# Two sets of level tiles for the block inverses, with rotary, key and value buffers shared or shortened

## The chip, the cores and the metric

The kernel runs on one core of one Trainium2 chip. The metric is the device time of one execution in microseconds; of several runs the median counts. The profile is of one execution of its own, whose time is given beside its span.

## The reference

One layer of a hybrid encoder in float32: 1024 tokens of width 1024. A first projection feeds two mixers, whose outputs are joined by an output projection; then come cross-attention to 256 memory tokens and a SwiGLU. The change lies in the first mixers.

```python
# (A) windowed attention: 8 query heads, 2 key/value heads of width 64, +-128 tokens
q, k = _rope(q, positions), _rope(k, positions)      # two rotated halves of 32
scores = einsum(q, k in the band) * 64 ** -0.5       # softmax with a sink logit per head
o = p / denom @ v
# (B) bidirectional gated DeltaNet: 4 heads of width 128, two directions
lower = where(strict, (k * beta) @ k.T * decay, 0)   # per chunk of tokens
sol = triangular_solve(lower + eye, [v * beta, k * beta * exp(g)])
scan over the chunks: v_new = u - w @ state; o = qg @ state + qk @ v_new
                      state = state * g_last + kg.T @ v_new
```

## The kernel before

Weights are split on the fly into a high and a low fp32r part, and every projection is three matmuls in place of one (`pg`, L261). The program is written as a list of stages, and a scheduler sets the order of the instructions on each engine from the dependences and its own cost model; the text of the program sets only the order in which stages are offered to it, as three strings. Every engine runs its list in order; loads and stores are nearly all issued by SyncE (SP).

In the first string the four DeltaNet heads are projected, convolved and prepared (`prep`), and `base_inverse` inverts the 32 x 32 diagonal blocks of each chunk's triangular matrix for a pair of heads g (heads 0 and 1, then 2 and 3). It does so on VectorE in 60 small steps, after a mask on GpSimd (POOL, L528), and stores the blocks to `d_inv` (L543). The second string is the stage of this change. Its letters are: L, the levels of a head; G, a gate projection; A, a rotary projection (A4 the keys, A0 to A3 the queries); V, the values; W, two attention windows. The third is the scan over the chunks (`psc`, L785), with the memory's keys and values and the remaining windows in between; it reads what the levels stored to `d_pz`.

`levels(h)` joins the 32 x 32 inverses of a head into 64 x 64 and then 128 x 128 ones. It fetches the diagonal blocks by twenty small loads (L551) into five tiles: `m5`, and D5, D6, Z0, Z1, which hold 128 x 128 blocks per chunk, zero outside the blocks. These four are allocated once, zeroed by GpSimd (L719), and used by all four heads in turn; so a head's fetches wait until the head before has stored its Z tiles to `d_pz` (L610). For each half of the chunks it also loads `Ul` (L572), transposes it (L576), masks it into L5 and L6, and does four rounds of small matmuls (L585 and L591), each evacuated before the next.

`attn_proj` multiplies a projection with the sine (`sn`) and cosine (`rop`), brings the sine product to the other half of each head by four copies on SP (`rot`, L734), adds, splits into `qhi` and `qlo`, and stores these to `d_q` or `d_k`. `value_proj` copies the values to `vT` (L746), transposes them (`ptv`, L749) and splits them into `vhl`. `window_keys(g)` loads a key group's `khi` and `klo` (L679); a window loads its queries `qs` (L625), and its matmuls are `psw`, `ptw` and `pow`.

Of the kernel before, what the change touches and what calls it, by code (L numbers as in the profile page):

```python
# [10 lines left out]
F32 = mybir.dt.float32  # L11
F32R = mybir.dt.float32r
# [7 lines left out]
P = 128  # L20
S = 1024
D = 1024
KT = D // P
NT = S // P
HALF = 512
# [7 lines left out]

ORDER_1 = "D0 P0 D1 P1 D2 B0 P2 D3 P3 B1".split()
ORDER_2 = "L0 L1 G0 G1 A4 V A0 A1 L2 L3 W W W A2 A3 G2 G3 W".split()
ORDER_3 = ("M " + "s01 W K " * 5 + "s01 K " * 3 + "s01 V V").split()
# [37 lines left out]
def tile_hybrid_block(  # L76
# [16 lines left out]
    def f32(ap):  # L93
        return ap.bitcast(F32)

    def bc(ap, axis, shape):
        return ap.unsqueeze(axis).to_broadcast(list(shape))

    def split(hi, lo, src, scale=None, eng=None):

        if scale is None:
            nc.scalar.copy(hi, src)  # L102
            (eng or nc.vector).tensor_tensor(lo, src, f32(hi), ALU.subtract)  # L103
        else:
            nc.scalar.activation(hi, src, AF.Identity, scale=scale)
            nc.vector.scalar_tensor_tensor(lo, src, scale, f32(hi), ALU.mult, ALU.subtract)

    def pool(name, bufs, **kw):
        return tc.tile_pool(name=name, bufs=bufs, reuse_waits="tile", **kw)
# [39 lines left out]
    trp = p1.enter_context(pool("trp", 2, side="right"))  # L149
# [48 lines left out]
    def small():  # L198
        return ps.tile([P, 512], F32, tag="ps", name="ps")
# [11 lines left out]
    for hf in range(2):  # L211
        hi = hx.tile([P, KT, HALF], F32R, name=f"hhi{hf}")
        lo = hx.tile([P, KT, HALF], F32R, name=f"hlo{hf}")
        for j in range(4):
            t = 4 * hf + j
# [48 lines left out]
    def proj(src_cols, eng=None):  # L264
        whi, wlo = load_w(src_cols, KT, P, eng)
        pp = [pg.tile([P, 512], F32, tag="pg", name="pg") for _ in range(2)]
        gemm_b(whi, wlo, hT, pp)
        return pp
# [140 lines left out]
    def together(gens):  # L409

        gens = list(gens)
        while gens:
            gens = [g for g in gens if next(g, g) is not g]
# [132 lines left out]
    def levels(h):  # L546

        g, hh = h // 2, h % 2

        def fetch(dst, q, i, d):  # L550
            nc.sync.dma_start(dst, d_inv[g][i][d, hh, :, q].rearrange("c r s -> r c s"))  # L551

        m5 = tl_.tile([P, NT, 32], F32, tag="m5", name="m5", bufs=1)
        D5a, D6a, *Za = wide_sets[0]
        for q in range(4):
            r = slice(32 * q, 32 * q + 32)
            fetch(m5[r], q, 1, 1 - q % 2)
            fetch(D5a[r, :, r], q, 0, q % 2)
            fetch(D6a[r, :, r], q, 0, q // 2)
            for d in range(2):  # L560
                fetch(Za[d][r, :, r], q, 1, d)

        def part(b):
            c4 = slice(4 * b, 4 * b + 4)

            def wide(name):
                return tl_.tile([P, 4, P], F32, tag=name, name=name, bufs=2)

            L5, L6 = wide("L5"), wide("L6")
            D5, D6, Z = D5a[:, c4], D6a[:, c4], [z[:, c4] for z in Za]  # L570
            Ul = wide("Ul")
            nc.sync.dma_start(Ul, d_u[g][hh, c4].rearrange("c p n -> p c n"))  # L572
            yield
            p_ = small().rearrange("p (c n) -> p c n", c=4)
            for j in range(4):
                nc.tensor.transpose(p_[:, j, :], Ul[:, j, :], ident)  # L576
            nc.vector.tensor_tensor(L5, p_, bc(cm["m5"], 1, (P, 4, P)), ALU.mult)
            nc.vector.tensor_tensor(L6, p_, bc(cm["m6"], 1, (P, 4, P)), ALU.mult)

            def pair(lt, mv, dd, w):  # L580

                yield
                p_ = small()[:, 0:4 * w].rearrange("p (c n) -> p c n", c=4)
                for c in range(4):
                    nc.tensor.matmul(p_[:, c, :], lt[:, c, :], mv[:, c, :], start=True, stop=True)  # L585
                bs = tl_.tile([P, 4, 64], F32, tag="bs", name="bs", bufs=2)[:, :, 0:w]
                nc.scalar.copy(bs, p_)
                yield
                p_ = small()[:, 0:4 * w].rearrange("p (c n) -> p c n", c=4)
                for c in range(4):  # L590
                    nc.tensor.matmul(p_[:, c, :], dd[:, c, :], bs[:, c, :], start=True, stop=True)  # L591
                return p_

            p_ = yield from pair(L5, m5[:, c4, :], D5, 32)
            z5 = tl_.tile([P, 4, 32], F32, tag="z5", name="z5", bufs=2)
            nc.scalar.mul(z5, p_, -1.0)
            nc.vector.transpose(D6[32:64, :, 0:32], z5[0:32])
            nc.vector.transpose(D6[64:96, :, 96:128], z5[96:128])
            nc.vector.tensor_copy(Z[1][32:64, :, 0:32], z5[32:64])
            nc.vector.tensor_copy(Z[0][64:96, :, 96:128], z5[64:96])  # L600
            mov6 = tl_.tile([P, 4, 64], F32, tag="mov6", name="mov6", bufs=2)
            nc.scalar.copy(mov6[0:64], Z[1][0:64, :, 0:64])
            nc.vector.tensor_copy(mov6[64:128], Z[0][64:128, :, 64:128])
            nc.scalar.copy(Z[0][0:32, :, 32:64], z5[0:32])
            nc.scalar.copy(Z[1][96:128, :, 64:96], z5[96:128])
            p_ = yield from pair(L6, mov6, D6, 64)
            nc.scalar.mul(Z[0][0:64, :, 64:128], p_[0:64], -1.0)
            nc.vector.tensor_scalar(Z[1][64:128, :, 0:64], p_[64:128], -1.0, None, ALU.mult)
            for d in range(2):
                nc.sync.dma_start(d_pz[g][d][c4, :, hh, 1].rearrange("c p n -> p c n"), Z[d])  # L610

        together([part(b) for b in range(2)])
# [60 lines left out]
    keys, vhl = {}, None  # L673

    def window_keys(g):
        keys[g] = tw.tile([P, S], F32R, tag="khi", name="khi"), tw.tile([P, S], F32R, tag="klo", name="klo", bufs=1)
        for kk, src in zip(keys[g], d_k):
            for r in range(2):
                nc.sync.dma_start(f32(kk[64 * r:64 * r + 64]), src[64 * g:64 * g + 64, :])  # L679
# [23 lines left out]
    def issue(order, table):  # L703
        for o in order:
            table[o[0]](*(int(c) for c in o[1:]))

    issue(ORDER_1, {"D": delta_proj, "P": lambda h: prep(h, *kqv[h]), "B": base_inverse})
    pp_.close()
# [3 lines left out]
    ps = pgs.enter_context(pool("psl", 2, space=PSUM))  # L712
    tw = p12.enter_context(pool("tw", 2))
    tw.tile([P, 384], F32, tag="sc", name="sc", bufs=8)
    vhl = tw.tile([P, NT + 1, 2, 2, 64], F32R, tag="vhl", name="vhl", bufs=1)[:, 0:NT]
    tl_ = p1.enter_context(pool("tl", 2))
    wide_sets = [[tl_.tile([P, NT, P], F32, tag=f"{n}{i}", name=n, bufs=1) for n in ("D5", "D6", "Z0", "Z1")] for i in range(1)]
    for t in wide_sets[0]:
        nc.gpsimd.memset(t, 0.0)  # L719

    def attn_proj(ct):
        pp = proj(w_in[:, ct * P:(ct + 1) * P])
        dst = [t[ct * P:(ct + 1) * P, :] if ct < 4 else t for t in (d_q if ct < 4 else d_k)]
        for hf in range(2):
            sl = slice(hf * HALF, (hf + 1) * HALF)
            rop = trp.tile([P, HALF], F32, tag="rop", name="rop")
            sn = trp.tile([P, HALF], F32, tag="rot", name="sn")
            rot = trp.tile([P, HALF], F32, tag="rot2", name="rot2")
            nc.vector.tensor_tensor(sn, pp[hf], sinT[:, sl], ALU.mult)
            nc.vector.tensor_tensor(rop, pp[hf], cosT[:, sl], ALU.mult)  # L730

            for q in range(4):
                o = 32 * (q ^ 1)
                nc.sync.dma_start(rot[32 * q:32 * q + 32], sn[o:o + 32])  # L734
            nc.vector.tensor_tensor(rop, rop, rot, ALU.add)
            hl = [trp.tile([P, HALF], F32R, tag=t, name=t) for t in ("qhi", "qlo")]
            split(*hl, rop)
            for t, o in zip(hl, dst):
                nc.sync.dma_start(o[:, sl], f32(t))
# [13 lines left out]
    def gate_proj(h):  # L753

        pp = proj(w_in[:, 2304 + h * P:2304 + (h + 1) * P])
        for hf in range(2):
            gt = trp.tile([P, HALF], F32, tag="rop", name="gt")
            nc.scalar.activation(gt, pp[hf], AF.Silu)
            nc.sync.dma_start(d_gate[h * P:(h + 1) * P, hf * HALF:(hf + 1) * HALF], gt)

    issue(ORDER_2, {"A": attn_proj, "V": value_proj, "G": gate_proj, "L": levels, "W": next_windows})
    dump("d_q", d_q); dump("d_k", d_k); dump("d_gate", d_gate)
    p1.close()
# [439 lines left out]
    for e in range(EARLY):  # L1203
        f = 2 * e
# [320 lines left out]
```

## Time and profile before

| | us |
|---|---|
| median of 3 runs | 1550.36 (1548.67 to 1551.51) |
| profiled execution, time | 1555.78 |
| profiled execution, span | 1554.1 |
| TensorE busy | 1497.3 |
| VectorE busy | 1055.9 |
| ScalarE busy | 719.6 |
| GpSimd busy | 308.3 |

The mean granted TensorE clock is 0.983. In the views quoted below, PE is TensorE and PEld its weight loads, DVE VectorE, ACT ScalarE, POOL GpSimd, SP SyncE; SPq is the queue of SyncE, that is, its DMA issues. A row of the chain gives start, length, engine, tile and line. A row of a line's instructions gives the shortest, median and longest duration in ns and the start of the first and the last. A tile is named in the profile without its number, and D5 and D6 both read D there.

### The profile page before, as it was taken

To read this page: it belongs to the slowest core of one execution; us is meant where nothing else is said; L and a number is where in the kernel's file an instruction comes from. 1 tells how busy PE (TensorE), PEld (TensorE's weight loads), DVE (VectorE), ACT (ScalarE), POOL (GpSimd) and SP (SyncE) were. 2 spreads that over 40 slices of the span, in tenths; PEclk is the share of its full clock that TensorE was granted. 3 is DMA by queue.
4 is the path that set the end of the run, shared out by engine and by line. 5 is a ranking of instruction groups with operands and counts; after the bars stand their busy time and mean duration, and the time that the engine had idled before them with its cause. 6 is when DMAs were issued, how large, how long until landed. Compare 5 with 4: busy or idle time off the path is not lost.

```text
span 1554.1 us, 20931 instructions
## 1 busy us (share of the span) xinstructions
PE 1497.3 (96%) x7451; PEld 1258.1 (81%) x7451; DVE 1055.9 (68%) x1750; ACT 719.6 (46%) x1380; POOL 308.3 (20%) x305
## 2 busy tenths in 40 slices
PE   6999999898899999999999999999999999999998
PEld 5888888787899877888888777888888888888786
DVE  6777898766898766443447367776867554687665
ACT  6666552246556755454335574332323332454532
POOL 2000110000003201163102221433533333000021
PEclk9999999997999999999999999999999999999999
DMA  6244456867987584354213264344434334863354
GB/s 211 69 136 128 125 157 160 217 179 245 319 278 247 164 283 165 119 190 148 82 55 123 85 200 141 111 135 129 134 122 132 102 102 141 288 193 102 108 175 165
DMA packets 267366, 247.16 MB, mean 159 GB/s; under 512 B 39016, under 2 KB 204797, under 8 KB 267261
## 3 DMA queue, kind: packets, MB, share of 16 engines
q1 hardware_dynamic: 267261, 245.82, 50.7%
q8 instruction: 59, 0.97, 0.3%
q14 instruction: 46, 0.38, 0.1%
HBM read 173.65 MB, written 69.50 MB: 156 GB/s over the span
## 4 chain that ended last, share of the span: by engine, by line
PE 80%; DVE 6%; DMA 6%; ACT 3%; issue 2%; SPq 2%; POOL 0%; DVEq 0%; POOLq 0%; ACTq 0%
PE pg L261 13%; PE pmg L1016 10%; PE pD L1196 8%; PE pE L1196 8%; PE pA L1196 6%; PE pcq L261 6%; PE pdX L1386 6%; PE pdA L1386 4%; PE pB L1196 4%; PE psc L785 2%; PE pdX L1479 2%; PE pdD L1386 2%; DMA wraw<-in_w_ckv_dram 2%; PE pcs L1102 1%; PE pco L1128 1%
## 5 line engine op out<-in xcount | busy, mean ns | idle before, releaser
L102 ACT CAST whi<-wraw 128x1024 fp32r<-128x1024 f32 x108 | 113.5, 1051 | 173.3 <-PE pg L261 36.0
L103 DVE TENSOR_TENSOR wlo<-wraw,whi 128x1024 fp32r<-128x1024 f32 x78 | 95.5, 1225 | 77.7 <-ACT whi L102 75.0
L261 PE MATMUL pg<-hhi,whi 128*128 128x512 f32 x352 | 140.8, 401 | 0.2 <-DVE rop L730 0.2
L261 PE MATMUL pg<-hhi,wlo 128*128 128x512 f32 x352 | 140.2, 399 | 0.0
L261 PE MATMUL pg<-hlo,whi 128*128 128x512 f32 x352 | 139.9, 398 | 0.0
L1016 PE MATMUL pmg<-whi,b 128*128 128x512 f32 x384 | 118.4, 394 | 0.4 <-ACT b L102 0.4
L1196 PE MATMUL pA<-s,whi 128*128 128x512 f32 x352 | 109.5, 392 | 1.4 <-ACT m L1213 1.4
L103 POOL TENSOR_TENSOR wlo<-wraw,whi 128x1024 fp32r<-128x1024 f32 x30 | 73.8, 2460 | 143.3 <-ACT whi L102 143.2
L1016 PEld LDWEIGHTS pmg<-whi,b 128*128 128x128 f32 x384 | 71.3, 188 | 15.2 <-ACT b L102 1.3
L261 PEld LDWEIGHTS pg<-hhi,whi 128*128 128x128 f32 x352 | 67.3, 192 | 14.0 <-DVE rop L730 0.7
L261 PEld LDWEIGHTS pg<-hlo,whi 128*128 128x128 f32 x352 | 67.2, 191 | 13.2
L261 PEld LDWEIGHTS pg<-hhi,wlo 128*128 128x128 f32 x352 | 67.2, 191 | 13.1
L1196 PEld LDWEIGHTS pA<-s,whi 128*128 128x128 f32 x352 | 65.3, 188 | 15.2 <-ACT m L1213 2.0
L1386 PE MATMUL pdX<-dhl,whi 128*128 128x512 f32 x264 | 76.1, 390 | 1.5 <-DVE zv L1441 0.8
L1016 PE MATMUL pmg<-wlo,b 128*128 128x512 f32 x192 | 71.5, 392 | 0.0
L1196 PE MATMUL pA<-s,wlo 128*128 128x512 f32 x176 | 68.7, 392 | 1.1 <-DVE wlo L103 1.1
L102 ACT CAST whi<-araw 128x1024 fp32r<-128x1024 f32 (+1 forms) x36 | 35.4, 984 | 69.9 <-PE pdX L1386 27.6
L1273 POOL TENSOR_TENSOR act<-act,up 128x512 f32<-128x512 f32 x33 | 50.1, 1519 | 89.1 <-DVE up L1272 53.1
L103 DVE TENSOR_TENSOR wlo<-araw,whi 128x1024 fp32r<-128x1024 f32 (+1 forms) x36 | 40.8, 1133 | 38.4 <-ACT whi L102 38.3
L286 DVE SCALAR_TENSOR_TENSOR acc<-cp,cols,acc 128x1024 f32<-128x1024 f32 x48 | 61.5, 1282 | 1.5 <-ACT acc L284 0.8
L1386 PEld LDWEIGHTS pdX<-dhl,whi 128*128 128x128 f32 x264 | 49.3, 188 | 12.8 <-issue 1.1
L1246 DVE TENSOR_TENSOR sr<-sr,wraw 128x512 f32<-128x512 f32 x22 | 37.8, 1716 | 29.8 <-POOL sr L1245 29.8
(409 smaller groups left out, 3976.7 us busy)
## 6 DMA issues: line engine op xcount, KB each, us to landing
wraw<-in_w_gate_up_dram SPq DMA_DIRECT2D x52, 512.0 KB, 4.0
kv<-d_kv SPq DMA_DIRECT2D x32, 512.0 KB, 6.6
wraw<-in_w_in_dram SPq DMA_DIRECT2D x22, 512.0 KB, 5.5
b<-in_w_down_dram SPq DMA_DIRECT2D x20, 512.0 KB, 6.8
araw<-d_as SPq DMA_DIRECT2D x20, 512.0 KB, 3.8
pz<-d_pz SPq DMA_DIRECT2D x32, 256.0 KB, 6.8
wraw<-in_w_ckv_dram SPq DMA_DIRECT2D x16, 512.0 KB, 6.4
wraw<-in_w_out_dram SPq DMA_DIRECT2D x16, 512.0 KB, 4.3
```

The source lines that it names most:

```text
L102: nc.scalar.copy(hi, src)
L103: (eng or nc.vector).tensor_tensor(lo, src, f32(hi), ALU.subtract)
L261: nc.tensor.matmul(p_, w[:, k, :], ah[a][:, k, :], start=(k == 0 and i == 0), stop=(k == nk - 1 and i == 2))
L286: nc.vector.scalar_tensor_tensor(acc, cp[:, t:t + S], taps[t], acc, ALU.mult, ALU.add)
L785: nc.tensor.matmul(out[:, d, h, :], lt[:, d, h, :], rt[:, d, h, :], start=True, stop=True)
L1016: nc.tensor.matmul(pp[t], act[a][:, k, tt], w_[:, kk, :], start=(k == 0 and i == 0), stop=(k == KT - 1 and i == 2))
L1102: nc.tensor.matmul(pp[:, t2_, :], q[a][:, ct, tt], kr_[b_][:, ct, :], start=(j == 0 and i == 0), stop=(j == 1 and i == 2))
L1196: nc.tensor.matmul(out_, w[a][:, k, :], xx[b_][:, k, :], start=(start and k == 0 and i == 0), stop=(k == HK - 1 and i == 2), skip_group_ch ...
L1246: nc.vector.tensor_tensor(s[1], s[0], a_[:, 0:HK], ALU.subtract)
L1273: nc.gpsimd.tensor_tensor(o_, o_, up, ALU.mult)
L1386: nc.tensor.matmul(banks[t], a[:, k - k0, tt], w, start=(first and k == 0 and i == 0), stop=(k == NB - 1 and i == 2), skip_group_check=not ...
L1479: nc.tensor.matmul(X[t], a[:, k], w[:, k0 + k], start=False, stop=(k0 + k == NB - 1 and i == 2), skip_group_check=True)
```

## The change

There are two sets of D5, D6, Z0 and Z1, and head h uses set h % 2: eight tiles are zeroed in place of four. To make room, L5, L6 and Ul take their slots from one tag with five slots, where they had two each; qhi and qlo take slots of the tags "rot" (which sn and vT use) and "rot2" (which the rotated copy uses), and have none of their own; khi has one buffer, as klo has; and vhl loses a slot that it did not use. Line numbers behind the new constant are one higher.

```diff
+LT = 5
...
-        D5a, D6a, *Za = wide_sets[0]
+        D5a, D6a, *Za = wide_sets[h % 2]
...
-                return tl_.tile([P, 4, P], F32, tag=name, name=name, bufs=2)
+                return tl_.tile([P, 4, P], F32, tag="L", name=name, bufs=LT)
...
-        keys[g] = tw.tile([P, S], F32R, tag="khi", name="khi"), tw.tile([P, S], F32R, tag="klo", name="klo", bufs=1)
+        keys[g] = tw.tile([P, S], F32R, tag="khi", name="khi", bufs=1), tw.tile([P, S], F32R, tag="klo", name="klo", bufs=1)
...
-    vhl = tw.tile([P, NT + 1, 2, 2, 64], F32R, tag="vhl", name="vhl", bufs=1)[:, 0:NT]
+    vhl = tw.tile([P, NT, 2, 2, 64], F32R, tag="vhl", name="vhl", bufs=1)
...
-    wide_sets = [[tl_.tile([P, NT, P], F32, tag=f"{n}{i}", name=n, bufs=1) for n in ("D5", "D6", "Z0", "Z1")] for i in range(1)]
-    for t in wide_sets[0]:
+    wide_sets = [[tl_.tile([P, NT, P], F32, tag=f"{n}{i}", name=n, bufs=1) for n in ("D5", "D6", "Z0", "Z1")] for i in range(2)]
+    for t in wide_sets[0] + wide_sets[1]:
         nc.gpsimd.memset(t, 0.0)
...
-            hl = [trp.tile([P, HALF], F32R, tag=t, name=t) for t in ("qhi", "qlo")]
+            hl = [trp.tile([P, HALF], F32R, tag=t, name=n) for t, n in (("rot", "qhi"), ("rot2", "qlo"))]
```

The scheduler orders the whole stage anew; the number of instructions stays what it was on every engine but GpSimd, which has four memsets more. Before and behind the stage (until the transposes of the first Ul, and from the output projection on) the order is the same. Three places follow.

On TensorE, the levels of head 0. Before, the two transposes of Ul (L576) lie 95 projection matmuls ahead of these rows, and the first two rounds look so, with projection matmuls (`pg`) between the rounds; `ptv` are the transposes of the values:

```order
L585 MATMUL ps<-m_2128,L_2153 128x32 x4
L261 MATMUL pg<-hhi_146,whi 128x512
L261 MATMUL pg<-hlo_147,whi 128x512
L261 MATMUL pg<-hhi_146,wlo 128x512
```

Six such projection matmuls stand there, and the rows go on:

```order
L591 MATMUL ps<-bs,D_2120 128x32 x4
L749 MATMUL ptv<-ident,vT 128x128 x4
L261 MATMUL pg<-hhi_232,whi 128x512
L261 MATMUL pg<-hlo_233,whi 128x512
L261 MATMUL pg<-hhi_232,wlo 128x512
L591 MATMUL ps<-bs,D_2120 128x32 x4
```

Now, behind 108 projection matmuls:

```order
L262 MATMUL pg<-hhi_146,wlo 128x512
L577 MATMUL ps<-ident,Ul 128x128 x8
L586 MATMUL ps<-m_2136,L_2157 128x32 x4
L586 MATMUL ps<-m_2136,L_2161 128x32 x4
L592 MATMUL ps<-bs,D_2120 128x32 x8
L586 MATMUL ps<-mov_2204,L_2158 128x64 x4
L586 MATMUL ps<-mov_2220,L_2162 128x64 x4
L592 MATMUL ps<-bs,D_2121 128x64 x8
L750 MATMUL ptv<-ident,vT 128x128 x4
L262 MATMUL pg<-hhi_232,whi 128x512
```

The transposes of Ul have moved to the levels, and no projection matmul is left between the rounds of head 0.

On SP, behind the fetches of head 0 (D, Z and m are the level tiles, with 2120 to 2123 the first set and 2124 to 2127 the second). Before, the copies for the second half of the keys' rotation follow soon behind the fetches; Ul in these rows is head 1's:

```order
L551 DMA Z_2123<-d_inv_112 32x8x32
L572 DMA Ul<-d_u_109 128x4x128 x2
L734 DMA rot_2552<-sn 32x512 x4
L734 DMA rot_2568<-sn 32x512 x2
L551 DMA m_2249<-d_inv_112 32x8x32 x4
L739 DMA d_k_100<-qhi 128x512
L739 DMA d_k_101<-qlo 128x512
L734 DMA rot_2568<-sn 32x512 x2
```

Now the first Ul rows behind the fetches are head 0's own, fourteen fetches of the second set for head 1 follow them, and the last of those and what comes behind are:

```order
L552 DMA D_2125<-d_inv_111 32x8x32
L552 DMA m_2257<-d_inv_112 32x8x32 x4
L552 DMA Z_2126<-d_inv_112 32x8x32
L552 DMA Z_2127<-d_inv_112 32x8x32
L573 DMA Ul<-d_u_109 128x4x128 x2
L740 DMA d_k_101<-qlo 128x512
L735 DMA rot_2576<-sn 32x512 x3
L126 DMA wraw<-in_w_in_dram 128x8x128
```

Three copies of the second half's rotation now stand behind the fetches of both heads, and Ul of head 0 stands behind its twenty fetches.

On SP, heads 1 and 2. Before, the stores of head 1's Z tiles (L610) stand ahead of the fetches of head 2 into the same tiles:

```order
L625 DMA qs<-d_q_98 64x4x128
L625 DMA qs<-d_q_99 64x4x128
L734 DMA rot_3557<-sn 32x512
L610 DMA d_pz_105<-Z_2122 128x4x128
L610 DMA d_pz_106<-Z_2123 128x4x128
L610 DMA d_pz_105<-Z_2122 128x4x128
L610 DMA d_pz_106<-Z_2123 128x4x128
L551 DMA D_2121<-d_inv_113 32x8x32 x3
L551 DMA Z_2122<-d_inv_114 32x8x32 x2
```

Now head 2's fetches into the first set stand ahead of head 1's stores of the second:

```order
L552 DMA D_2121<-d_inv_113 32x8x32
L552 DMA Z_2122<-d_inv_114 32x8x32
L552 DMA Z_2123<-d_inv_114 32x8x32
L573 DMA Ul<-d_u_110 128x4x128
L740 DMA d_q_98<-qhi 128x512
L611 DMA d_pz_105<-Z_2126 128x4x128
L740 DMA d_q_99<-qlo 128x512
L611 DMA d_pz_106<-Z_2127 128x4x128
```

The fetches of a head have moved ahead of the stores of the head before; the fetches of head 3 follow right behind head 1's stores, and the weights of the last two gate projections (`wraw`), which before stood ahead of head 2's last fetches, stand behind them.

## The prediction

> **What bounds the kernel now.** I read the page first (engines, then the chain by engine), then a table of windows over the stage that the change touches, then the waits of TensorE there and the chain of that stretch. The profiled execution took 1555.78 us, of which 1554.1 us are the span; that is 5.4 us above the median of 1550.36 us, so a change worked out on the trace is carried over to the median as a difference, not as a ratio. A measurement of this kernel can tell about 0.2%, or 3.1 us, from no change.
>
> ```profile
> PE 1497.3 (96%) x7451; PEld 1258.1 (81%) x7451; DVE 1055.9 (68%) x1750; ACT 719.6 (46%) x1380; POOL 308.3 (20%) x305
> PE 80%; DVE 6%; DMA 6%; ACT 3%; issue 2%; SPq 2%; POOL 0%; DVEq 0%; POOLq 0%; ACTq 0%
> ```
>
> TensorE (PE) is busy 96% of the span and carries 80% of the chain. Nothing in the diff changes how many matmuls there are. So the change can only move time through TensorE's idle time and through the slow clock that follows it, and only between the first levels and the end of the scan. The table by stage (columns: stretch and its length, busy us and instructions of PE, PEld, DVE, ACT and POOL, granted clock, DMA share, GB/s) shows what there is to gain:
>
> ```profile
> 240.00:260.00 20.00, 17.97 (x91) 15.38 (x91) 17.48 (x42) 5.09 (x13) 2.26 (x1) 0.91 0.55 128
> 260.00:280.00 20.00, 20.00 (x104) 16.87 (x103) 18.00 (x40) 4.91 (x10) 0.00 (x0) 0.92 0.85 247
> 280.00:300.00 20.00, 18.94 (x107) 16.11 (x106) 16.48 (x37) 6.41 (x16) 0.16 (x1) 1.00 0.69 176
> 300.00:320.00 20.00, 16.13 (x77) 13.58 (x77) 8.01 (x18) 3.20 (x6) 0.00 (x0) 0.83 0.84 192
> 340.00:360.00 20.00, 20.00 (x124) 17.66 (x121) 14.39 (x34) 12.73 (x27) 0.20 (x1) 1.00 0.90 257
> 250.00:260.00 10.00, 7.97 (x46) 7.18 (x46) 8.10 (x21) 4.03 (x12) 0.00 (x0) 0.83 0.63 172
> 312.00:320.00 8.00, 8.00 (x31) 6.73 (x32) 3.98 (x11) 0.00 (x0) 0.00 (x0) 0.63 0.67 164
> 366.00:372.00 6.00, 6.00 (x26) 5.68 (x25) 2.81 (x7) 1.44 (x4) 0.00 (x0) 0.50 0.31 87
> 372.00:378.00 6.00, 3.99 (x13) 2.36 (x11) 2.46 (x10) 5.66 (x14) 0.20 (x1) 0.50 0.80 220
> 378.00:383.00 5.00, 3.81 (x14) 3.30 (x14) 4.27 (x12) 2.44 (x5) 1.95 (x4) 0.52 0.98 366
> ```
>
> Lost TensorE time is the idle time plus the busy time multiplied by what is missing from the clock. Before, three places lose: about 2.0 + 1.4 = 3.4 us at 250 to 260; 3.9 us idle at 300 to 320 and 8 x 0.37 = 3.0 us of clock behind it; and at 366 to 383, just ahead of the scan, 3.0 + (2.0 + 2.0) + (1.2 + 1.8) = 10.0 us. The largest sum that the change could win in its stage, were all three to go, is therefore about 21 us with the 1.1 us of 280 to 300. The chain says what ended these waits (start, length, what):
>
> ```profile
> 234.78 14.96 PE pg L261 x66
> 249.74 0.87 PE ps L585 x8
> 253.03 2.03 DMA rot<-sn
> 255.80 0.66 PE ptv L749 x4
> 269.89 0.84 PE ps L591 x8
> 276.66 4.43 DMA d_pz<-Z
> 296.75 5.34 DMA d_q<-qhi
> 306.21 5.30 DMA qs<-d_q
> 355.25 4.63 DMA d_gate<-gt
> 359.89 2.87 DMA Z<-d_inv
> 369.08 1.60 PE ps L591 x8
> ```
>
> Two of these rows are the shared level tiles: the Z fetch of head 1 stands behind the stores of head 0 (276.66), and head 3's Z fetch (359.89) behind those of head 2. The stall at 306 to 311, however, is a window's query load, and the one at 253 is a rotary load.
>
> **Part by part: the order of issue.** Four more memsets cost POOL four times the row below. In the new order, all eight stand behind the second diagonal mask (L528) instead of ahead of it; the mask starts at 241.3.
>
> ```profile
> L719 POOL MEMSET D<- x2: 947/948/950, 212.8 to 213.7; 128x1024 f32 x2
> L528 POOL TENSOR_SCALAR_AFFINE_SELECT A<-A x2: 1773/2014/2256, 164.0 to 241.3; 128x1024 f32<-128x1024 f32 x2
> L551 SPq DMA_DIRECT2D m<-d_inv x16: 320/467/1333, 238.6 to 325.6; - x16
> L551 SPq DMA_DIRECT2D Z<-d_inv x32: 302/449/1042, 240.4 to 359.9; - x32
> L734 SPq DMA_DIRECT2D rot<-sn x40: 507/588/1240, 251.1 to 340.6; - x40
> L572 SPq DMA_DIRECT2D Ul<-d_u x8: 360/397/451, 221.0 to 320.8; - x8
> DMA to landing us min/median/max: 2.7/3.2/3.7
> ```
>
> 241.3 + 2.3 + 8 x 0.948 = 251.2 on POOL: the memsets have no cover there, because head 0's fetches write the same tiles. The first tile is clear at 244.5 and the first set at 247.4, so the twenty fetches of head 0 (0.449 us of SP each, 9 us), which before began at 238.6, end near 255. The two Ul loads, which before were issued at 221, are now issued behind them, at about 255, and land 3.2 us later, at about 258.4. TensorE reaches the transposes of Ul at 249.74 + 13 x 0.227 - 1.3, or about 251.4: thirteen more projection matmuls (14.96 / 66 = 0.227 us each) stand ahead of them, and the two groups of transposes (0.66 us each, by the row of 255.80) that were done early are still to do. It waits there until 258.4, and then has the whole of head 0's levels back to back, eight groups of four matmuls at 0.84 us (8 in the trace, as each takes two passes) and the transposes, 8.0 us in all, each waiting for a copy, with no projection matmul between them.
>
> Next in TensorE's order come the transposes of the values, whose vT now takes a "rot" slot that it shares with a rotary product and a qhi. The three missing rotary copies stand behind some 25 more issues on SP, which are Ul, the set-1 fetches of head 1 and a key store. That is 256 + 25 x 0.449 = 267.2 for the first; the third is issued at 268.4 and lands 2 to 3 us later, by the row of 253.03. With the copy to vT, TensorE goes on at about 272.9. So some 22 us hold about 8 us of work: 14 us idle, where before had 2. By the order of instructions, the changed kernel is then 35 projection matmuls (8.0 us) and two groups of value transposes (1.3 us) behind, or 9.3 us.
>
> A clock term follows the stall. In the rows, 312 to 320 was at 0.63 after a 3.9 us wait, a loss of 3.0 us; before has 1.4 us of it at the same place. I take 2 us more. [...]
>
> **Part by part: the second set of tiles.** It pays from head 1 on. The second base inverse is a chain of sixty small steps on VectorE (DVE), and shared DVE before with evacuations of the levels and rotary sums: 17.48, 18.00 and 16.48 us busy of 20 from 240 on. In the new order that other work waits with TensorE's stall while the steps go on, and by the rows of these steps the inverse's stores come at about 280 to 282.
>
> ```profile
> L543 SPq DMA_DIRECT2D d_inv<-V x4: 471/538/588, 228.6 to 292.8; - x4
> L543 SPq DMA_DIRECT2D d_inv<-A x4: 477/618/1101, 229.9 to 296.1; - x4
> L785 PE MATMUL psc<-kv,pz x128: 270/275/377, 382.8 to 515.1; 128*128 128x128 f32 x128
> ```
>
> Before, they came at up to 296.1, so they are some 14 us earlier. Head 2 is then fetched at once, at 284 to 304, where before its D6 and Z tiles were held by head 1's stores. Heads 2 and 3 then keep TensorE fed. The stall of 300 to 320 should go: 3.9 + 3.0 + 1.1 us are won, and 9.3 + 2.0 - 8.0 = 3.3 us remain behind at 320. From there to 366 before loses next to nothing (20.00 busy of 20 at 340 to 360), so nothing is won.
>
> Ahead of the scan, up to 10.0 us can be won. The floor, with all of it won, is a first scan matmul 10.0 - 3.3 = 6.7 us earlier than before's 382.8. What is late next is not head 3's fetch but the gate and rotary chain: the weights of the last two gate projections are issued only after head 3's fetches (before: ahead of head 2's), the rotary copies of the last two query columns stand behind head 2's stores, and head 3's stores must land before the scan's first load. Adding up these steps with the rows above, the last levels end near 367 (before 369.08 + 1.60 = 370.7), the stores go at 367 to 370, the first load is issued at about 374.5 and the scan starts at about 380: 3 us won, not 6.7.
>
> ```profile
> wraw<-in_w_in_dram SPq DMA_DIRECT2D x5, 512.0 KB, 5.8
> d_q<-qhi SPq DMA_DIRECT2D x7, 256.0 KB, 2.4
> PE psw L633 <- DMA qs<-d_q: 3.9, 1, 3.9
> PE ptv L749 <- ACT vT L746: 2.0, 1, 2.0
> ```
>
> **Part by part: the shared buffers.** L5, L6 and Ul with five slots in place of six, and qhi and qlo in the rotary slots, add waits on slots. The second is already in the walk above (vT, and each rotary product behind a store to d_q that lands 2.4 us after its issue). A weight load that is late is bounded by nothing below and by its 5.8 us above; nearest is the 3.9 us wait for a load of queries, and I take 3 us. One key buffer fewer holds the second key group's load behind window 7, but the other key tile already had one buffer: two issues, about 1 us. The spare value slot costs nothing, being never used.
>
> By the order of instructions, the windows lag: at the first scan matmul the changed kernel has about 3 us more of window work left (12 more transposes at 0.66 / 4 us, some value products, and a dozen memory transposes fewer). The scan also fills TensorE with that work, so it counts in full.
>
> **Sum.** -3 (the scan earlier) + 3 (window work left) + 1 (key loads) + 3 (late weights) = +4 us. On the execution of the trace this is 1555.78 + 4 = 1559.8 us, and on the median 1554.5 us.
>
> **The rivals.** *The scan starts at the floor* (faster). The late weights and the rotary chain cost nothing because the window matmuls cover them, and the scan starts 6.7 us earlier; the window work left over fits into what TensorE idles in the scan. Speaking for it: the two Z rows of the chain vanish, and 4.63 us of the 10 us ahead of the scan come from a store of gates that merely kept SP waiting. Against it: both windows and scan use the same TensorE. It gives -7 us, or -9 where the 2 us of clock after the stall do not come either; at -8, 1542.4 us. It decides where the last fetch of head 3 lands more than 5 us before TensorE wants it.
>
> *The stall is not won back* (slower by more). The 14 us wait at 251 to 273 stays lost, since the later waits are of queues, not of tiles: the query load of 306.21 and the gate store of 355.25 would come 9.3 + 2.0 us later with all that follows. Price: +11, up to +17 with the 5.8 us weight load; at 13 us, 1563.4 us. It decides where the waits for the queries and the gate store are as long as before although TensorE comes to them later. For it speaks that the two largest waits of TensorE in this stretch in the list of waits are a query load and vT, neither a level tile. Against it: 10 us lie idle before the scan. [...]
>
> *It doesn't do what it says*: the heads still wait for each other at TensorE, loss and gain cancel, and the time is within 3.1 us of before, 1550.4 us.
>
> **How the numbers follow.** Forecast +4 (its own range +1 to +8, 1551.4 to 1558.4): 0.40. Scan at the floor: 0.28. Stall not won back: 0.20. Cancelled: 0.12. Faster by over 0.2%: 0.26 of the second case and 0.05 of the forecast, should its late weights cost nothing and the scan gain more than taken, 0.31. Slower: the 0.20, 0.29 of the forecast and 0.03 of the last case, 0.52. Same: what is left, 0.17. The range reaches to the faster rival's 1541.4 (-9) and, for the stall kept with half of the load's 5.8 us, to +16, 1566.4.
>
> **What would show it.** In the changed profile: a wait of TensorE for Ul and vT of together 12 to 16 us between 250 and 274, and clock below 0.9 there; the second inverse's stores at about 281; no wait of 3.9 us for qs; head 3's Z fetches no longer behind a store of d_pz; the first scan matmul at 378 to 382; the output projection starting later by about as much as the time grows. The forecast is wrong if the stall at 251 is under 6 us, if the scan starts before 376 or after 386, or if the difference in time lies outside 227 to 600 us.

## The result and the profile after

The changed kernel takes 1568.19 us (median of 6 runs, 1565.59 to 1571.81) against 1550.93 us of the kernel before (6 runs): a ratio of 1.0113 with an interval of 1.0098 to 1.0129, or 17 us slower. The profiled execution took 1569.36 us with a span of 1567.6, 13.5 us above the span of before; the profiled execution of before lay some 5 us above its median, so the traces show 13.5 of the 17 us.

The first rows are a table of windows over the stage, of before and then of after (columns as in the prediction):

```profile
245.00:290.00 45.00, 42.97 (x227) 36.81 (x227) 37.61 (x92) 11.77 (x26) 0.16 (x1) 0.92 0.69 184
290.00:315.00 25.00, 20.07 (x104) 16.75 (x103) 14.48 (x29) 7.84 (x18) 0.00 (x0) 0.92 0.94 240
315.00:360.00 45.00, 44.77 (x259) 39.12 (x257) 31.13 (x79) 23.19 (x59) 0.99 (x3) 0.97 0.71 193
360.00:400.00 40.00, 33.06 (x181) 27.60 (x180) 27.34 (x75) 24.27 (x60) 2.55 (x7) 0.78 0.78 251
```

```profile
245.00:290.00 45.00, 34.35 (x158) 29.88 (x156) 38.56 (x95) 10.26 (x23) 6.89 (x9) 0.73 0.64 161
290.00:315.00 25.00, 25.00 (x143) 21.67 (x143) 15.91 (x31) 6.78 (x18) 0.00 (x0) 1.00 0.60 163
315.00:360.00 45.00, 36.85 (x175) 31.81 (x173) 16.56 (x45) 11.05 (x29) 0.20 (x1) 0.81 0.77 183
360.00:400.00 40.00, 36.54 (x210) 31.70 (x210) 27.46 (x71) 26.22 (x60) 2.61 (x7) 0.96 0.60 196
```

TensorE's loss, length less busy time multiplied by the clock, was 5.5, 6.5, 1.6 and 14.2 us in these four stretches, and is now 19.9, 0.0, 15.2 and 4.9. At 290 to 315 and ahead of the scan 15.8 us less are lost. Two new stalls cost 14.4 and 13.6 us. From 227 to 620 us the loss grows from 44.0 to 56.0 us, which is most of the 13.5 us.

The loss of before ahead of the scan seems to be in part that of its one profiled execution, whose 1555.78 us lie above all six timed runs (to 1552.25). The run below with khi at one buffer and padding has the matmuls of before in the same order, with only the key loads placed otherwise on SP, and the same median within 0.1%. In its profile the row is:

```profile
360.00:400.00 40.00, 33.16 (x213) 28.60 (x212) 29.92 (x82) 28.77 (x68) 2.55 (x7) 0.91 0.85 265
```

It loses 9.8 us there in place of 14.2: its mean clock in that row is 0.91, that of before 0.78, where it is at half for 17.1 us (365.7 to 382.8). The two spans are 1547.4 and 1554.1 us.

The rows of the two stalls, from the waits of TensorE and from the rows by line:

```profile
PE ps L577 <- DMA Ul<-d_u: 8.5, 2, 7.9
PE psw L634 <- DMA qs<-d_q: 6.7, 1, 6.7
L720 POOL MEMSET D<- x4: 946/947/952, 244.5 to 249.0; 128x1024 f32 x4
L573 SPq DMA_DIRECT2D Ul<-d_u x8: 440/460/1224, 257.1 to 327.1; - x8
L750 PE MATMUL ptv<-ident,vT x8: 270/347/422, 278.2 to 284.0; 128*128 128x128 f32 x8
L544 SPq DMA_DIRECT2D d_inv<-A x4: 477/798/1121, 230.8 to 285.9; - x4
L786 PE MATMUL psc<-kv,pz x128: 270/276/421, 397.3 to 527.6; 128*128 128x128 f32 x128
```

The zeroing begins at 244.5, Ul is issued at 257.1, and TensorE waits 7.9 us for it. The levels of head 0 then run with nothing between them, from 260.2 to 278.2. The value transposes come at 278.2, in place of 255.8; TensorE doesn't wait for vT, which is copied at 275.9. The second stall is in SP's queue; the rows of its timeline (start, length, what):

```profile
320.87 2.00 SPq L552 DMA_DIRECT2D D<-d_inv  x2
322.92 0.94 SPq L552 DMA_DIRECT2D Z<-d_inv  x2
323.90 0.94 SPq L552 DMA_DIRECT2D D<-d_inv  x2
324.89 0.94 SPq L552 DMA_DIRECT2D Z<-d_inv  x2
325.88 0.49 SPq L680 DMA_DIRECT2D khi<-d_k  x1
...
329.42 2.60 SPq L626 DMA_DIRECT2D qs<-d_q  x4
332.61 0.38 SPq L126 DMA_DIRECT2D wraw<-in_w_in_dram  x1
```

The fetches of head 3, which now wait for head 1's stores and no longer for head 2's, stand in front of the first window's keys and queries and of the weights. TensorE runs out of projection matmuls at 330.3 and waits to 337.0. The scan starts at 397.3, in place of 382.8.

### The profile page after: what moved, and what is told of

Its sections match the earlier page's. It is cut to its first block, busy times and chain, and to the rows that moved or that the text cites. A ratio compares the mean times of both kernels' runs of the same rounds, so it can differ in the third digit from the quotient of the medians.

```text
span 1567.6 us, 20952 instructions
## 1 busy us (share of the span) xinstructions
PE 1502.3 (96%) x7451; PEld 1263.7 (81%) x7451; DVE 1061.5 (68%) x1750; ACT 718.6 (46%) x1380; POOL 315.2 (20%) x309
## 4 chain that ended last, share of the span: by engine, by line
PE 64%; DVE 4%; ACT 3%; DMA 2%; issue 2%; POOL 1%; SPq 0%; DVEq 0%; POOLq 0%; ACTq 0%
PE pmg L1017 10%; PE pD L1197 7%; PE pE L1197 7%; PE pA L1197 6%; PE pcq L262 6%; PE pdX L1387 6%; PE pdA L1387 4%; PE pB L1197 4%; PE psc L786 3%; PE pdD L1387 2%; PE pcs L1103 1%; PE pco L1129 1%; PE pdX L1480 1%; PE pow L665 1%; PE pck L917 1%
## 5 line engine op out<-in xcount | busy, mean ns | idle before, releaser
L262 PEld LDWEIGHTS pg<-hhi,wlo 128*128 128x128 f32 x352 | 66.8, 190 | 13.5
```

Source lines behind the costliest of these rows:

```text
L262: nc.tensor.matmul(p_, w[:, k, :], ah[a][:, k, :], start=(k == 0 and i == 0), stop=(k == nk - 1 and i == 2))
```

## The experiments

All times are medians beside the kernel before in the same batch; the bracket behind a ratio is its interval. Losses are worked out as above.

**Which part of the change costs.** First all edits but the second set:

```diff
-        D5a, D6a, *Za = wide_sets[h % 2]
+        D5a, D6a, *Za = wide_sets[0]
...
-... for i in range(2)]
-    for t in wide_sets[0] + wide_sets[1]:
+... for i in range(1)]
+    for t in wide_sets[0]:
```

> All the edits that make room, but one set of level tiles, as before. Theory P (placement): khi and vhl shrink the window pool by 5 KB per partition, so the level tiles move down onto tiles of the preparation whose last stores go out late; zeroing, fetches and Ul come late whether there are one or two sets. It expects TensorE's wait for Ul at about 251 to 258 again and 1558 to 1570 us. Theory S (slots): qhi and qlo in the rotary slots hold vT and the rotary sums; also slow here, with the wait on vT larger than that on Ul. Theory T (two sets): the second head's fetches fill SP's queue ahead of the rotary copies; it expects no more than 3 us off the kernel before (1548 to 1554).

Measured: 1575.72 us, ratio 1.0168 (1.0143 to 1.0192), and a wait for Ul of 7.8 us. Making room costs all of the loss and more, without a second set; theory T, as the sole cause, falls. The two-set kernel is 8 us faster than this one, but not in its own stage: the scan starts at 395.6 here and at 397.3 there, and a wait of 6.4 us of the output projection for VectorE, behind the scan, stands in this run alone. Within the stage the second set costs: TensorE's wait for the first window's queries is 1.4 us here and 6.7 us there, and the loss at 315 to 360 is 8.7 us here and 15.2 us there.

Then single edits, on the kernel before. Only khi and vhl shorter:

```diff
-... name="khi"), tw.tile(...
+... name="khi", bufs=1), tw.tile(...
-    vhl = tw.tile([P, NT + 1, 2, 2, 64], ...)[:, 0:NT]
+    vhl = tw.tile([P, NT, 2, 2, 64], ...)
```

> The kernel before with only khi at one buffer and vhl without its spare slot: the level tiles lie 5 KB lower, nothing else. P expects the late zeroing (behind the second mask on GpSimd, at about 244 instead of 213), Ul behind the fetches, a TensorE wait of 5 us or more between 245 and 265, and 8 to 17 us more than before. S and T expect no difference at 250 and at most 3 us in all, for the key load.

Measured: 1573.24 us, ratio 1.0151 (1.0133 to 1.0169). The same short khi, with 4 KB of padding to keep the place:

```diff
-... name="khi"), tw.tile(...
+... name="khi", bufs=1), tw.tile(...
+    tw.tile([P, S], F32, tag="pad", name="pad", bufs=1)
```

> The kernel before with khi at one buffer and 4 KB of padding in its place, so that all level tiles lie where they lay. If the 23 us of the run with khi and vhl shortened come from where the level tiles lie (theory P), this one is within 4 us of the kernel before; if they come from the key load that can no longer be made ahead (theory K), it is 10 us or more slower, with a wait of TensorE on khi.

Measured: 1549.37 us, ratio 0.9993 (0.9979 to 1.0006). The pair differs in the place of the level tiles, by 5 KB per partition, and in vhl's unused slot, which no instruction touches. The zeroing, first with the tiles moved down and then with padding:

```profile
L719 POOL MEMSET D<- x2: 952/952/952, 244.6 to 245.5; 128x1024 f32 x2
```

```profile
L720 POOL MEMSET D<- x2: 951/952/952, 212.7 to 213.6; 128x1024 f32 x2
```

So the place costs 24 us by itself, and the key load that can't be made ahead costs nothing that shows. Why the place sets the order is inferred, not shown: the tiles moved down would lie on tiles of the preparation, of which `pm`, for one, is stored to `d_pz` as late as 237 to 239. What the trace shows is that the zeroing stands behind the second mask in GpSimd's order and follows it without a gap (with the tiles moved down, the mask takes 1.7 us from 243.0 and the zeroing begins at 244.6). With one set or two, Ul then follows the fetches. These are the changed kernel's stores, in SP's timeline, and the largest wait of TensorE up to 400 us in the run with the tiles moved down:

```profile
237.16 1.76 SPq L424 DMA_DIRECT2D d_pz<-pm  x3
```

```profile
PE psw L633 <- DVE m L635: 8.7, 2, 8.3
```

The path that theory P gave is not what cost the time in that run. TensorE waits 0.2 us for Ul there, in place of the 5 us or more that P expected, and the stretch of 245 to 290 loses only 7.8 us; TensorE stands 8.3 us at a window later, whose scores wait on VectorE, and 13.5 us are lost at 315 to 360.

Only qhi and qlo in the rotary slots:

```diff
-            hl = [trp.tile([P, HALF], F32R, tag=t, name=t) for t in ("qhi", "qlo")]
+            hl = [trp.tile([P, HALF], F32R, tag=t, name=n) for t, n in (("rot", "qhi"), ("rot2", "qlo"))]
```

> The kernel before with only qhi and qlo moved into the rotary slots. S expects 8 to 15 us more, with the wait for vT at 253 grown from 2 us to 8 or more. P expects zeroing at 213 and Ul at 221 as before and within 4 us of the kernel before.

Measured: 1567.56 us, ratio 1.0117 (1.0098 to 1.0135): as much as the whole change, with zeroing and Ul as early as before. The value transposes come at 282.8, and 21.6 us are lost at 245 to 290. The wait for vT is 3.0 us and not the 8 or more that S expected; larger are two waits of the levels, for `mov`, the copy that feeds the next round (6.9 us), and for m5 (5.0 us). Place is thus one cause of two, and either edit is enough.

Only L5, L6 and Ul in one tag of five slots:

```diff
-                return tl_.tile([P, 4, P], F32, tag=name, name=name, bufs=2)
+                return tl_.tile([P, 4, P], F32, tag="L", name=name, bufs=LT)
```

> The kernel before with only L5, L6 and Ul in one tag of five slots. It costs little by all theories so far: zeroing and Ul as early as before, within 4 us of the kernel before. A difference over 8 us would mean that any new order of this stage is worse than the one of before (theory O), whatever tile it is that is short.

Measured: 1556.77 us, ratio 1.0044 (1.0026 to 1.0062): 7 us, more than was expected, and less than theory O's line. TensorE's largest wait there is again for a window's queries, 6.8 us, with one set of tiles: three of the first window's four loads stand behind head 2's fetches. So a second set is not the only edit that can put fetches ahead of these loads.

**Taking the place away.** The changed kernel, with the second set in a pool of its own below:

```diff
+    tl1 = p1.enter_context(pool("tl1", 1))
     tl_ = p1.enter_context(pool("tl", 2))
-    wide_sets = [[tl_.tile(...) ...] for i in range(2)]
+    wide_sets = [[p_.tile(...) ...] for i, p_ in enumerate((tl_, tl1))]
```

> The changed kernel with the second set in a pool of its own, allocated below the other level tiles: the same tiles and slots, but only the second set lies on the preparation's late tiles. P expects zeroing of the first set near 213, Ul at about 221, no wait for Ul at 251, and 1543 to 1553 us. S and T expect the stall of 251 to 273 to stay and 1560 us or more.

Measured: 1571.4 us, ratio 1.0142 (1.0117 to 1.0167). Ul was issued at 217.7 and no wait for it stood at 251, and still 22.9 us were lost at 245 to 290: waits for VectorE's `mov` (6.3 us) and for m5 (4.7 us) took its place. P is not enough for the changed kernel.

Two sets of Z alone, so that qhi and qlo keep their slots, and the second pair below:

```diff
...
+    wide_sets.append(wide_sets[0][:2] + [tl1.tile(...) for n in ("Z0", "Z1")])
...
+            hl = [trp.tile([P, HALF], F32R, tag=t, name=t) for t in ("qhi", "qlo")]
```

> Two sets of Z0 and Z1 only, the second pair in a pool of its own below; D5 and D6 stay single, and qhi and qlo keep their own slots; khi, vhl and the L tag as in the change. Neither the low place of the first set nor the shared rotary slots are left. P and S together expect the stall at 251 to 273 to be gone and the gain of the second set (about 8 us against the run with one set) to show: 1540 to 1552 us. Theory O expects 1558 us or more.

Measured: 1556.41 us, ratio 1.0051 (1.0034 to 1.0068). With both costs out, 10 of the 17 us are gone. What is left is about what the L tag costs alone, and a gain of a second set does not show.

**Taking single waits away.** Ul ahead of the fetches, in the changed kernel:

```diff
         D5a, D6a, *Za = wide_sets[h % 2]
+        Uls = []
+        for b in range(2):
+            Uls.append(tl_.tile([P, 4, P], F32, tag="L", name="Ul", bufs=LT))
+            nc.sync.dma_start(Uls[b], d_u[g][hh, 4 * b:4 * b + 4].rearrange("c p n -> p c n"))
```

> The changed kernel with the two Ul loads of a head written ahead of its twenty fetches. If the wait for Ul (7.9 us) is itself the loss, the time falls by 5 to 8 us to 1560 to 1563. If the levels of head 0 only wait for the next late thing, as in the run with the second set placed apart, TensorE's idle time of 245 to 275 is the same and the time is within 4 us of the changed kernel's 1568.

Measured: 1572.34 us, ratio 1.0145 (1.0125 to 1.0165), and 18.5 us lost at 245 to 290 in place of 19.9: removing the wait for Ul wins no time. That wait is gone, and these now head the list (waits of TensorE up to 400 us):

```profile
PE ps L589 <- DMA m<-d_inv: 6.2, 2, 4.3
PE ps L580 <- DVE Z L612: 5.4, 3, 4.5
```

The windows' loads ahead of head 3's fetches:

```diff
-... "L0 L1 G0 G1 A4 V A0 A1 L2 L3 W W W A2 A3 G2 G3 W"
+... "L0 L1 G0 G1 A4 V A0 A1 L2 W W W L3 A2 A3 G2 G3 W"
```

> The changed kernel with the second string written L2 W W W L3: the order up to the first windows is the changed kernel's, word for word, but the first windows' keys and queries stand on SP ahead of head 3's fetches, no longer behind them. If the second stall (315 to 360 us, 15 us of TensorE time) is those loads queued behind fetches made early by the second set (theory Q), the first window's matmul comes at about 327 in place of 337, the wait for qs goes, and the time falls by 6 to 12 us to 1556 to 1562. If the stall only moves to the next late thing, the time is within 4 us of 1568.

Measured: 1566.56 us, ratio 1.0107 (1.0092 to 1.0123). The first window's matmul comes at 323.7 in place of 337.0, and the loss at 315 to 360 falls from 15.2 to 10.6 us, but at 360 to 400 it grows from 4.9 to 8.9. The wait for the queries falls from 6.7 to 2.9 us and is not gone; the scan starts at 399.6. Theory Q has the place of the wait right and its price wrong. The same edit of the string in the two-Z version and in the kernel before:

> The version with two sets of Z alone, the second pair in its own pool below, and the string L2 W W W L3. Theory Q: its 4.3 us wait for qs goes, and with it 4 to 8 us of 1556: 1548 to 1553. Otherwise 1555 or more.

> The kernel before with the string L2 W W W L3, as a control: there head 2's and 3's fetches wait for stores in any case, and the first windows' loads already stand ahead of head 3. Theory Q expects no more than 4 us of difference either way; a gain like that of the two-set versions would mean that the order of the string, not the second set, is what the two-set runs gained.

Measured: 1559.68 us, ratio 1.0062 (1.0040 to 1.0084), no better than 1.0051, and its wait for the queries grew from 4.3 to 5.7 us, where theory Q had it gone; and 1549.78 us, ratio 1.0004 (0.9991 to 1.0016). The string is not what decides.

**The shared slots.** More of them, with only qhi and qlo moved; three, and in a second kernel four, for sn, rot2, vT, qhi and qlo:

```diff
-            sn = trp.tile([P, HALF], F32, tag="rot", name="sn")
+            sn = trp.tile([P, HALF], F32, tag="rot", name="sn", bufs=3)
...
```

> As the run with only qhi and qlo in the rotary slots, but with three slots each in place of two. Theory S in its narrow form: with two slots only one half column is in flight, so the next half's copies wait for the store of the half before, a pitch of 7 to 8 us per half where TensorE makes a half in 5.4 us. A third slot lets the next half start: rotary copies no longer one half at a time, and 8 us or more of the 17.8 us come back (1550 to 1559). Theory O (any other order of this stage is slower): 1562 or more.

> The same with four slots each: as much memory as before, pooled otherwise. Narrow S: within 4 us of the kernel before (1546 to 1554). Theory O: 1558 or more.

Measured: 1568.39 us, ratio 1.0123 (1.0102 to 1.0143), and 1569.95 us, ratio 1.0129 (1.0111 to 1.0147). Four slots are as much memory as before, and nothing comes back, as theory O expects and S does not: the number of slots is not the cause. What stayed is the order of SP's rows. In the timeline of the run with four slots:

```profile
261.40 2.50 SPq L734 DMA_DIRECT2D rot<-sn  x4
268.38 0.52 SPq L734 DMA_DIRECT2D rot<-sn  x1
278.69 1.78 SPq L734 DMA_DIRECT2D rot<-sn  x3
```

Three of the four copies of the keys' second half go 10 us behind the first. In the changed kernel it is 24 us (246.3 and 270.7). Two sets of Z as above, with the shared tags at three slots and no L tag:

```diff
...
+            hl = [trp.tile([P, HALF], F32R, tag=t, name=n, bufs=3) for t, n in (("rot", "qhi"), ("rot2", "qlo"))]
...
+                return tl_.tile([P, 4, P], F32, tag=name, name=name, bufs=2)
```

> Two sets of Z alone with the second pair in its own pool below, qhi and qlo in rotary tags of three slots, L5, L6 and Ul with two slots each as before; khi and vhl short. If a third slot pays for the sharing and the L tag cost the 7 us that it cost alone, this is the best version with a second set: 1544 to 1552. If the third slot does not, 1558 or more.

Measured: 1571.71 us, ratio 1.0137 (1.0121 to 1.0153): the late copies again, 20.5 us lost at 245 to 290.

**The rotary copies first.** One edit, in four versions:

```diff
-                nc.sync.dma_start(rot[32 * q:32 * q + 32], sn[o:o + 32])
+                with tc.high_priority(AHEAD):
+                    nc.sync.dma_start(rot[32 * q:32 * q + 32], sn[o:o + 32])
```

> The changed kernel with the rotary copies put in the scheduler's order ahead of the level fetches that are not yet due (priority on these copies alone). Theory R: the slow versions have in common that the last three copies of the keys' second half stand behind some 25 fetches, so vT is late, the projection accumulators stay full and head 0's levels run without other work. The copies now stand two rows behind head 0's fetches, so R expects the three copies before 262 in place of 271, vT before 268 in place of 277, and 5 to 10 us less than 1568. If memory (place and slots) delays it anyhow, within 4 us of 1568.

> Both full sets, the second in its own pool below, and the rotary copies ahead. R: the copies come with head 0's fetches at 250 to 256, TensorE's loss at 245 to 290 falls from 23 us to under 10, and the time from 1571 to 1553 to 1560. Otherwise 1566 or more.

> Only qhi and qlo in the rotary slots, and the rotary copies ahead. R: the loss at 245 to 290 falls from 22 us to under 10 and the time from 1567.6 to 1552 to 1558. If the shared slots hold vT in any order, 1564 or more.

> Two sets of Z alone with the second pair below, own slots for qhi and qlo, and the rotary copies ahead. R expects its loss at 245 to 290 (11 us) to fall to the 5 us of before and the time to 1546 to 1553, at best a little under the kernel before; otherwise 1555 or more.

Measured: 1564.12 us, ratio 1.0099 (1.0079 to 1.0118); 1576.23 us, 1.0179 (1.0158 to 1.0199); 1562.99 us, 1.0089 (1.0069 to 1.0109); 1567.0 us, 1.0116 (1.0088 to 1.0145). In the changed kernel the three copies go at 258.3 and the value transposes at 267.7, as R has it, and the loss at 245 to 290 falls from 19.9 to 15.5 us; yet the ratio stays within the interval of the changed kernel's. In the second version 22.2 us are lost there and in the third 15.8 us, both over R's 10. In the last version the first stretch is healed, and this is what takes its place (value transposes, then the largest wait of TensorE up to 400 us):

```profile
L753 PE MATMUL ptv<-ident,vT x8: 272/374/454, 254.9 to 261.0; 128*128 128x128 f32 x8
PE psw L634 <- DMA qs<-d_q: 7.7, 1, 7.7
```

Only 6.7 us are lost at 245 to 290, and 13.3 at 315 to 360, for the queries behind the fetches of heads 2 and 3. R falls as a way to get the time back.

What is shown: the lower place costs 24 us by itself and the shared tags 17.8 us by themselves; the costs don't add, as both together with the L tag cost 26 us, and with the second set 17. Removing any one late load leaves the next. What stays open is by which link the place and the L tag change the order, and why four shared slots, as many as before, lead to the late copies: the order is the scheduler's, and no run took the order of before into that kernel. Of the nine further versions with a second set none was faster than the kernel before.

## Why the prediction was wrong

The sign was right and the size was not: +4 us was forecast with a range to +16, and +17 came. The rival that the stall is not won back, at +11 to +17 and with a chance of 0.20, came closest. That its upper price fits is luck in part: it took 5.8 us of it from a late weight load, and no wait for weights stands in TensorE's list for the stage. Of the waits that it named, the one for the queries stayed and grew, from 3.9 to 6.7 us, but the loss just ahead of the scan fell.

- *The first stall* was foreseen where it came, and from Ul: the zeroing was put to end at 251.2 and ended at 251.7, and Ul, put at about 255, was issued at 257.1. Idle time at 245 to 290 is 10.65 us, against the 14 of the sum. But the levels of head 0, put at 8.0 us, took 18.0 (260.2 to 278.2), all at half clock. So TensorE took up the values at 278.2 and not at 272.9, and for vT, the second half of the foreseen wait, it did not wait at all.
- *The clock term* of that stall is the first that was mis-sized. It was 2 us more; measured is 9.3 us (19.9 of loss less 10.65 idle), against 3.4 before. Of these 3.4 the prediction counted 1.4; its own row of 260 to 280, at 0.92, holds 1.6 us more. The clock stood at half for 20 us behind the wait, all through the levels (below); the 3.0 us that the term was taken from came from a row with projection matmuls behind the wait. The whole stall cost 14.4 us more than before, where 9.3 and 2.0 were booked.
- *"The stall of 300 to 320 should go"* failed. The second set let head 2's fetches go earlier, but TensorE's wait there was for a window's queries, as the prediction's own rows said. The early fetches of head 3 moved ahead of these queries on SP, and the wait of 3.9 us became one of 6.7 us at 330 to 337, with the clock at half from 335.4 to 352.5. That is the step that cost most: 8.0 us were booked as won, and over 290 to 360 the loss went from 8.1 to 15.2 us.
- *The second inverse* came at 284.6 to 285.9 (forecast 280 to 282, before 292.2 to 296.1): 10 us earlier where 14 were forecast.
- *The scan* was to start at 380 and starts at 397.3. The losses ahead of the scan did fall, by 9.3 us at 360 to 400, but the kernel came to 360 us some 21 us behind (35.1 of loss against 13.6). Nor were the 10.0 us all there to win, it seems: against the run with padding, which has the same order of matmuls and loses 9.8 us there, the fall is 4.9.
- *The other terms* of the sum, 7 us of window work, key loads and late weights, don't show. The scan starts 14.5 us later and the output projection (`pmg`) 14.6 us later, at 584.3 in place of 569.7, so in the traces the whole miss lies ahead of the scan. A key buffer fewer cost nothing in the run with padding.
- *The shared buffers* were costed, beyond the walk, at 1 us for the key loads and 3 us for late weights, with the spare value slot named as costing nothing. Alone, the 5 KB lower place costs 24 us, and the shared tags 17.8 us; the L tag alone costs 7 us. The walk priced their effect on the order once, at head 0, and not on what the scheduler does behind it.

## What to carry to other kernels

Where a scheduler sets the order, memory is a term of it: a pool 5 KB lower cost 24 us here. Before buffers are shortened to make room, look which earlier tiles the next pool comes to lie on, and when their last reader is done. A buffer that lets loads go earlier lets them go ahead of loads that are needed sooner, where one engine issues all of them; look what stands behind them in that queue. An idle window later on is not a reserve that wins a stall back, unless what ends it moves too. And a loss that one execution shows may be that execution's clock (ahead of the scan, 14.2 us were lost at a mean clock of 0.78 and 9.8 us at 0.91, with the matmuls in the same order): before it is counted as there to win, look for it in a second profile of the same order.

## What the runs showed of the hardware

In the changed kernel the clock stood at half behind the wait for Ul, of 7.9 us, while TensorE was nearly always busy, but with small dependent matmuls (columns as above):

```profile
260.00:264.00 4.00, 3.52 (x15) 2.77 (x15) 2.70 (x5) 0.00 (x0) 0.00 (x0) 0.50 0.54 91
264.00:268.00 4.00, 4.00 (x20) 4.00 (x21) 3.69 (x11) 0.53 (x2) 0.00 (x0) 0.50 0.33 52
268.00:272.00 4.00, 3.30 (x16) 3.19 (x16) 3.64 (x13) 2.55 (x8) 0.00 (x0) 0.50 0.60 145
272.00:276.00 4.00, 3.29 (x16) 3.13 (x16) 3.70 (x12) 1.34 (x4) 0.00 (x0) 0.50 0.88 271
276.00:280.00 4.00, 4.00 (x19) 3.81 (x19) 2.80 (x10) 1.73 (x5) 0.15 (x1) 0.50 0.68 220
280.00:284.00 4.00, 4.00 (x23) 3.34 (x22) 3.83 (x6) 0.00 (x0) 0.00 (x0) 0.90 0.83 223
```

```profile
262.69 3.59 PE L586 MATMUL ps<-m,L 128*128 128x32 f32 x16 [0.16 <-PE ps L577]
...
278.91 0.78 PE L262 MATMUL pg<-hhi,whi 128*128 128x512 f32 x1
...
281.25 0.39 PE L262 MATMUL pg<-hhi,whi 128*128 128x512 f32 x1
```

It stood at 0.50 for 20 us, 18.1 of them busy, in which only level rounds and transposes ran until 278.9; from 264 to 268 TensorE had no idle time at all by the trace. The projection matmuls of 512 columns, which began at 278.91 (the rows are of TensorE's timeline), were at their full pace some 2 us later: the first took 0.78 us, that of 281.25 took 0.39 us. In the stall of before the clock came back at 263.3, 4.4 us after projection matmuls had begun to run alone, at 258.94. In the changed kernel it stayed at half through 64 rows of level matmuls of 32 and 64 columns, with a weight load each, which the trace shows as 14.3 us busy. Whether their size, the weight loads or gaps too short for the trace had a part in it, no run shows.

Behind the second stall, of 6.7 us, the clock stood at half from 335.4 to 352.5, with some larger matmuls, of 256, 384 and 512 columns, among the rounds.

In the packed traces of before and of the changed kernel the granted clock has two values, 1.0 and 0.5. The stretches at half, but for the one that the end cuts off, last 6.83, 6.83, 17.07, 6.83, 6.83 and 3.41 us in before, and 23.89, 17.07, 3.41, 6.83 and 3.41 us in the changed kernel: to 0.01 us, each is 1, 2, 5 or 7 times 3.413 us.
